# Attention logits of both maps made together, each map in its own 64 rows of the PE array

## The chip, the cores and the metric

One core of one Trainium2 chip runs the whole program. The metric is device time in microseconds. Engines are named as in the profile: PE is TensorE (with PEld, its weight loads), DVE is VectorE, ACT is ScalarE, POOL is GpSimd, SP issues most DMAs.

## The reference, cut to what matters

A two-layer trunk over 1024 tokens of width 1024. The change touches the second layer's differential attention: 8 heads, each with two maps (r = 0, 1) of 64 dimensions and values of 128.

```python
def diff_attention(qkv, q_gain, k_gain, lam_params, sub_gain, lam_init):
    q = rms_norm(q.reshape(bsz, seq, C_HEADS, 2, 64), q_gain) * 64 ** -0.5
    k = rms_norm(k.reshape(bsz, seq, C_HEADS, 2, 64), k_gain)
    v = v.reshape(bsz, seq, C_HEADS, 128)
    ...
        logits = einsum('bqhrd,bkhrd->bhrqk', q_blk, k) - slopes * dist    # blocks of 128 queries
        probs = softmax(where(dist >= 0, logits, -inf), axis=-1)
        attn = probs[:, :, 0] - lam * probs[:, :, 1]
        return einsum('bhqk,bkhe->bqhe', attn, v)
    ...
    o = rms_norm(o, sub_gain) * (1.0 - lam_init)
```

Everything is float32. The logits and the projections are made from float32 numbers that are split in two parts, `hi` (rounded to the type float32r, which PE multiplies in one pass) and `lo` (the rest), with the product of the two `lo` parts left out.

## The kernel before

The program is one stream: the first layer's mixing stage, its MLP and gate, then `attention` (L872 on), then the output projection and the second MLP. A scheduler of the framework orders each engine's instructions from the program's dependencies and from simulated times. An engine's queue is then fixed, and it runs in order.

`attention` walks through 8 heads of 8 blocks of 128 queries, 64 blocks in all, plus two iterations to drain. Block `b` of a head sees `n = (b + 1) * 128` keys, in one chunk of up to 512 columns for b < 4 and in two (512 and the rest) for b > 3: 96 chunks for each map. In iteration g of the loop the source issues

- `logits(0)` of block g, then `combine` of block g-1,
- `transpose` of block g-2, `logits(1)` of block g, `value` of block g-2,

with a call of `pump` between them. `pump` issues units of the work that fills PE meanwhile: the projections for later heads (tile `mm`), and near the end a part of the output projection (`mix_part`).

**Parts of q and k.** `put_k` transposes 512 keys (both maps stand one above the other in the 128 rows of `pt`) and writes for each map r a tile of 128 rows: `hi` in the map's own 64 rows, `lo` in the other 64 (L969 on ACT, L970 on DVE, 64 rows each). `put_q` does the same for 256 queries, but puts `hi` in both halves of `qh` (L980 on ACT, copied across by L981 on DVE), and `lo` in the own half of `ql` (L982 on DVE), whose other half was set to zero once (L947).

**Logits.** So each chunk of a map takes two matmuls over all 128 rows into one PSUM tile `qk`: `qh` with `ks` gives hi·hi + hi·lo, and `ql` with `ks` gives lo·hi. L1016 on DVE adds the bias `al`, writes `lg` and keeps the running extreme `nm`; L1019 on ACT takes the exponential and the sums.

**After the logits.** `combine` (L1025 to L1027, DVE) joins the two maps, `transpose` puts the result in `aT` by way of PSUM (L1037, ACT), `value` multiplies by v in `po` (L1047, L1049).

**PSUM** has four tags of two banks each here: `mm`, `tr`, `aux` and `sc`. The logits' tiles cycle through `aux`, `sc`, `aux`; `po` lives in `sc`.

All matmuls of this stage use the whole 128x128 array. The first layer's mixing stage, around 195 to 380 us, has small ones of 32*32 and 64*64 (tiles `py`, `pz`). A float32 product that isn't split (`po`, `tr`, `py`, `pz`) shows in the trace as two instructions.

Of the kernel before, what the change touches and what calls it, by code (L numbers as in the profile page):

```python
# [12 lines left out]
F32R = mybir.dt.float32r  # L13
AF = mybir.ActivationFunctionType
ALU = mybir.AluOpType
# [3 lines left out]
P = 128  # L19
# [4 lines left out]
HT = 512  # L24
# [15 lines left out]
def f32(ap):  # L40
    return ap.bitcast(F32)
# [73 lines left out]
class Trunk:  # L115
# [756 lines left out]
    def attention(self, w_qkv, w_out, gain_next, h_dram):  # L872

        nc = self.nc
        NB = NT
        hs, r = list(self.hs), list(self.r)
        self.mixed = [[None] * KT, [None] * KT]

        al = self.slot("B", [P, S], F32, "al")
# [62 lines left out]
        half = (slice(0, 64), slice(64, P))  # L942


        qlow = [self.slot(t, [P, 2, 2 * P], F32R, "ql") for t in ("c13", "d0")]
        for t in qlow:
            nc.vector.memset(f32(t), 0.0)  # L947

        lgs = [self.slot(f"A{4 + i}", [P, 2, S], F32, "lg") for i in range(2)]
        lg0 = [lgs[0][:, 0], lgs[0][:, 1], lgs[1][:, 0]]  # L950
        lg1 = lgs[1][:, 1]
        qk_tag = itertools.cycle(("aux", "sc", "aux"))
        aT_tag = itertools.cycle(("c8", "c9", "c10"))
        heads = {}

        def begin(hd):

            qk = qks[hd]

            ks = self.slot(f"A{2 + hd % 2}", [P, 2, S], F32R, "ks")  # L960

            def put_k(hf):
                pt = self.aux([P, HT], "tr", "tr")
                for t in range(4):
                    self.pe.transpose(pt[:, t * P : (t + 1) * P], qk[1][hf][:, t, :], self.ident)
                for r in range(2):
                    own, other = half[r], half[1 - r]
                    dst = ks[:, r, hf * HT : (hf + 1) * HT]
                    nc.scalar.activation(dst[own], pt[own], AF.Copy, scale=self.kg[own])  # L969
                    nc.vector.scalar_tensor_tensor(dst[other], pt[own], self.kg[own], f32(dst[own]), ALU.mult, ALU.subtract)  # L970

            def put_q(b2):
                pt = self.aux([P, HT], "tr", "tr")
                for i in range(2):
                    self.pe.transpose(pt[:, i * P : (i + 1) * P], qk[0][b2 // 2][:, 2 * (b2 % 2) + i, :], self.ident)
                qh = self.slot(f"c{11 + b2 % 2}", [P, 2, 2 * P], F32R, "qh")
                ql = qlow[b2 % 2]
                for r in range(2):
                    own, other = half[r], half[1 - r]
                    nc.scalar.activation(qh[own, r], pt[own, 0 : 2 * P], AF.Copy, scale=self.qg[own])  # L980
                    nc.vector.tensor_copy(qh[other, r], f32(qh[own, r]))  # L981
                    nc.vector.scalar_tensor_tensor(ql[own, r], pt[own, 0 : 2 * P], self.qg[own], f32(qh[own, r]), ALU.mult, ALU.subtract)  # L982
                return qh, ql

            put_k(0)
            heads[hd] = [ks, put_k, put_q, put_q(0)]

        class Block:
# [10 lines left out]
                me.sums, me.osq = heads[hd][4:6]  # L999
                me.nm = self.sp.tile([P, 2, 2], F32, tag="nm", name=self.nm("nm"))  # L1000

            def logits(me, r):
                hd, b, n, nm, lg = me.hd, me.b, me.n, me.nm, me.lg[r]
                if b == 0 and r == 0:
                    nc.vector.tensor_scalar(al, al, 0.5, None, ALU.mult)
                ks, _, _, (qh, ql) = heads[hd][:4]
                qs = slice((b % 2) * P, (b % 2 + 1) * P)
                nch = (n + HT - 1) // HT
                u0 = (NB - 1 - b) * P
                for c in range(nch):  # L1010
                    k0, k1 = c * HT, min(n, (c + 1) * HT)
                    ps = self.aux([P, HT], next(qk_tag), "qk")
                    self.pe.matmul(ps[:, : k1 - k0], lhsT=qh[:, r, qs], rhs=ks[:, r, k0:k1], start=True, stop=False)
                    self.pe.matmul(ps[:, : k1 - k0], lhsT=ql[:, r, qs], rhs=ks[:, r, k0:k1], start=False, stop=True)

                    nc.vector.tensor_tensor_reduce(  # L1016
                        out=lg[:, k0:k1], in0=ps[:, : k1 - k0], in1=al[:, u0 + k0 : u0 + k1], scale=-1.0,
                        scalar=3.0e38 if c == 0 else nm[:, r, 0:1], op0=ALU.add, op1=ALU.min, accum_out=nm[:, r, c : c + 1])
                nc.scalar.activation(lg[:, :n], lg[:, :n], AF.Exp, bias=nm[:, r, nch - 1 : nch], scale=-1.0, accum_out=me.sums[:, b, r : r + 1])  # L1019

            def combine(me):
                b, n, sums = me.b, me.n, me.sums
# [86 lines left out]
        def pump():  # L1109
            i = state[0] = state[0] + 1  # L1110
            for (i0, u0), (i1, u1) in zip(marks, marks[1:]):
                if i0 < i <= i1:
                    want = u0 + (u1 - u0) * (i - i0) / (i1 - i0)
                    while state[1] < want:
                        next(fill)
                        state[1] += 1
            if i > TAIL:
                next(tail, None)
# [12 lines left out]
        tail = tails()  # L1131
        blocks = []
        for g in range(8 * NB + 2):
            if g < 8 * NB:
                hd, b = divmod(g, NB)
                blocks.append(Block(hd, b))
                blocks[g].logits(0)
            if 0 < g <= 8 * NB:
                blocks[g - 1].combine()
            pump()  # L1140
            if g < 8 * NB and b % 2 and b < NB - 1:
                q = heads[hd][2]((b + 1) // 2)
            if g > 1:
                blocks[g - 2].transpose()
            pump()
            if g < 8 * NB:
                if b == 3 - (hd < 7):
                    heads[hd][1](1)
                blocks[g].logits(1)
            pump()  # L1150
            if g > 1:
                blocks[g - 2].value()
            pump()
            if g < 8 * NB:
                if b % 2 and b < NB - 1:
                    heads[hd][3] = q
                if b == 6 + (hd == 6) and hd < 7:
                    begin(hd + 1)
# [824 lines left out]
```

## Time and profile before

| what | value |
|---|---|
| median of 3 runs | 2536.98 us (2535.73 to 2537.92) |
| span of the profiled execution | 2535.2 us |
| PE / PEld / DVE / ACT busy, share of the span | 99% / 85% / 73% / 51% |
| granted TensorE clock, mean | 0.999 |

The span is the time from the first to the last instruction of one profiled execution; it lies 1.8 us under the median of the runs. In the rows of the trace, the first number after "x count" or the second of a timeline row is a duration; matmuls are pipelined, so that their durations overlap, and the distance between two starts tells what one costs. The form of a matmul's row is rows*columns of the array, then partitions x columns of its output.

### The profile page before, as it was taken

How to read it: one execution, taken by the hardware profiler on the slowest of the kernel's cores; microseconds unless marked ns; L12 is line 12 of the kernel's file. 1: busy time of each engine (PE TensorE's matmuls, PEld its weight loads, DVE VectorE, ACT ScalarE, POOL GpSimd, SP SyncE). 2: the span in 40 equal slices, each digit the busy share in tenths (PEclk: the TensorE clock that was granted, in tenths of full speed). 3: DMA queues.
4: the chain of work that ended last, by engine and by line, in shares of the span. 5: the costliest groups of instructions: out<-in, count | busy, mean ns of one | idle time of the engine just before them, and what ended most of it. 6: DMA issues, size and time to landing. Idle time of an engine off the chain costs nothing.

```text
span 2535.2 us, 40147 instructions
## 1 busy us (share of the span) xinstructions
PE 2515.3 (99%) x14046; PEld 2151.9 (85%) x14046; DVE 1854.3 (73%) x3676; ACT 1285.9 (51%) x2553; POOL 285.5 (11%) x256
## 2 busy tenths in 40 slices
PE   9999999999999999999999999999999999999999
PEld 7898898888888878888999999988778888888877
DVE  7867776697666888656477777787887677787586
ACT  6543444465455434544366666665654555445452
POOL 0301232000000000000334333310000000000000
PEclk9999999999999999999999999999999999999999
DMA  7452435457557756553211111147466558655651
GB/s 242 126 157 78 136 110 193 138 175 242 161 174 257 245 164 207 183 158 120 74 53 47 55 47 43 59 136 257 143 219 202 174 184 281 216 184 185 200 178 59
DMA packets 298818, 396.92 MB, mean 157 GB/s; under 512 B 37780, under 2 KB 165752, under 8 KB 298616
## 3 DMA queue, kind: packets, MB, share of 16 engines
q1 hardware_dynamic: 298600, 394.36, 48.4%
q8 instruction: 110, 1.80, 0.3%
q14 instruction: 92, 0.75, 0.1%
q10 hardware_dynamic: 16, 0.00, 0.0%
HBM read 289.40 MB, written 104.86 MB: 156 GB/s over the span
## 4 chain that ended last, share of the span: by engine, by line
PE 92%; DVE 4%; DMA 2%; issue 1%; ACT 1%; SPq 0%; POOL 0%; DVEq 0%; ACTq 0%; POOLq 0%
PE mm L76 79%; PE po L76 3%; PE qk L76 2%; PE aux L76 2%; PE tr L79 2%; DMA raw<-in_w_ple_gate_dram 1%; DVE lg L1016 0%; DVE w L224 0%; DMA raw<-in_w_mlp_dram 0%; PE pz L76 0%; PE py L76 0%; PE aux L79 0%; PE pvn L76 0%; PE pab L79 0%; PE pkq L76 0%
## 5 line engine op out<-in xcount | busy, mean ns | idle before, releaser
L76 PE MATMUL mm<-g,w 128*128 128x512 f32 x2592 | 603.6, 394 | 0.8 <-DVE g L224 0.5
L223 ACT CAST w<-raw 128x512 fp32r<-128x512 f32 x598 | 366.0, 618 | 453.8 <-PE mm L76 386.8
L76 PEld LDWEIGHTS mm<-g,w 128*128 128x128 f32 x2592 | 485.9, 188 | 116.2 <-DVE g L224 1.0
L76 PE MATMUL mm<-hi,w 128*128 128x512 f32 x1728 | 553.6, 396 | 0.3 <-ACT hi L1219 0.3
L76 PE MATMUL mm<-w,hi 128*128 128x256 f32 (+2 forms) x2528 | 505.5, 295 | 0.0
L224 DVE TENSOR_TENSOR w<-raw,w 128x512 fp32r<-128x512 f32 x534 | 364.8, 690 | 178.9 <-ACT w L223 169.4
L76 PEld LDWEIGHTS mm<-w,hi 128*128 128x128 f32 x2528 | 400.1, 188 | 13.6 <-DVE acc L284 0.3
L76 PEld LDWEIGHTS mm<-hi,w 128*128 128x128 f32 x1728 | 324.7, 188 | 73.7 <-ACT hi L1219 0.7
L76 PE MATMUL mm<-w,lo 128*128 128x256 f32 (+2 forms) x1264 | 370.3, 293 | 0.0
L76 PE MATMUL mm<-lo,w 128*128 128x512 f32 x864 | 341.6, 396 | 0.9 <-DVE lo L1220 0.9
L76 PE MATMUL mm<-t,w 128*128 128x512 f32 x1152 | 270.9, 394 | 1.2 <-ACT w L223 1.2
L76 PEld LDWEIGHTS mm<-t,w 128*128 128x128 f32 x1152 | 216.2, 188 | 52.8 <-ACT w L223 1.6
L76 PEld LDWEIGHTS mm<-w,lo 128*128 128x128 f32 x1264 | 238.2, 188 | 5.6
L76 PEld LDWEIGHTS mm<-lo,w 128*128 128x128 f32 x864 | 162.8, 188 | 36.8 <-DVE lo L1220 1.4
L224 DVE TENSOR_TENSOR g<-graw,g 128x512 fp32r<-128x512 f32 x216 | 147.2, 685 | 8.8 <-DMA gd<-g 6.9
L223 ACT CAST g<-graw 128x512 fp32r<-128x512 f32 x216 | 132.7, 617 | 32.8 <-issue 10.9
L1019 ACT ACTIVATE lg<-lg,nm 128x128 f32<-128x128 f32 (+7 forms) x128 | 99.5, 777 | 82.5 <-DVE nm L1016 76.0
L260 POOL TENSOR_TENSOR r<-ms,mhalf 128x4 f32<-128x4 f32 x12 | 13.3, 1109 | 1060.9 <-DVE ms L258 1033.5
L350 ACT ACTIVATE g<-g 128x512 f32<-128x512 f32 x96 | 60.6, 632 | 114.8 <-DVE g L284 114.5
L1016 DVE CUSTOM_DVE_ANT_0 lg<-qk,al 128x512 f32<-128x512 f32 (+3 forms) x128 | 75.1, 589 | 36.2 <-PE qk L76 32.8
L224 POOL TENSOR_TENSOR w<-raw,w 128x512 fp32r<-128x512 f32 x64 | 84.6, 1347 | 111.9 <-ACT w L223 63.0
L76 PE MATMUL mm<-ohi,w 128*128 128x512 f32 x256 | 85.2, 400 | 0.5 <-ACT ohi L1073 0.5
(336 smaller groups left out, 3612.4 us busy)
## 6 DMA issues: line engine op xcount, KB each, us to landing
raw<-in_w_mlp_dram SPq DMA_DIRECT2D x352, 256.0 KB, 3.3
graw<-gd SPq DMA_DIRECT2D x224, 256.0 KB, 2.8
gd<-g SPq DMA_DIRECT2D x192, 256.0 KB, 3.1
raw<-in_w_ple_gate_dram SPq DMA_DIRECT2D x76, 256.0 KB, 3.5
acc<-h_dram SPq DMA_DIRECT2D x64, 256.0 KB, 4.4
keep<-in_w_mlp_dram SPq DMA_DIRECT2D x64, 256.0 KB, 4.3
raw<-in_w_in_e_dram SPq DMA_DIRECT2D x60, 256.0 KB, 3.7
h_dram<-acc SPq DMA_DIRECT2D x48, 256.0 KB, 2.5
```

Source lines behind the costliest of these rows:

```text
L76: self._next(self.engine.matmul(*a, **k))
L79: self._next(self.engine.transpose(*a, **k))
L223: self.nc.scalar.copy(hi, src)
L224: (lo_engine or self.nc.vector).tensor_tensor(lo, src, f32(hi), ALU.subtract)
L260: nc.gpsimd.tensor_tensor(r, ms, self.mhalf[:, 0:4], ALU.pow)
L350: nc.scalar.activation(g, src, AF.Relu)
L1016: nc.vector.tensor_tensor_reduce(out=lg[:, k0:k1], in0=ps[:, : k1 - k0], in1=al[:, u0 + k0 : u0 + k1], scale=-1.0, scalar=3.0e38 if c == 0 ...
L1019: nc.scalar.activation(lg[:, :n], lg[:, :n], AF.Exp, bias=nm[:, r, nch - 1 : nch], scale=-1.0, accum_out=me.sums[:, b, r : r + 1])
```

## The change

The parts of q are kept once: `qs[:, 0]` has `hi` and `qs[:, 1]` `lo`, of both maps in the rows in which the transposes leave them; `ks[:, 0]` and `ks[:, 1]` the same for k. `put_k` and `put_q` make each part in one instruction over 128 rows. A logits chunk takes three matmuls for each map (hi·hi, hi·lo, lo·hi), each over the map's own 64 rows, the two maps alternating in the source, into two PSUM tiles, one of `aux` and one of `sc`. `logits` makes both maps of a block in one call, behind the `combine` of the block before.

```diff
-        qlow = [self.slot(t, [P, 2, 2 * P], F32R, "ql") for t in ("c13", "d0")]
-        for t in qlow:
-            nc.vector.memset(f32(t), 0.0)
...
-        qk_tag = itertools.cycle(("aux", "sc", "aux"))
+        qk_tag = itertools.cycle(("aux", "sc"))
...
             def put_k(hf):
...
-                for r in range(2):
-                    own, other = half[r], half[1 - r]
-                    dst = ks[:, r, hf * HT : (hf + 1) * HT]
-                    nc.scalar.activation(dst[own], pt[own], AF.Copy, scale=self.kg[own])
-                    nc.vector.scalar_tensor_tensor(dst[other], pt[own], self.kg[own], f32(dst[own]), ALU.mult, ALU.subtract)
+                hi, lo = (ks[:, i, hf * HT : (hf + 1) * HT] for i in range(2))
+                nc.scalar.activation(hi, pt, AF.Copy, scale=self.kg)
+                nc.vector.scalar_tensor_tensor(lo, pt, self.kg, f32(hi), ALU.mult, ALU.subtract)
 
             def put_q(b2):
...
-                qh = self.slot(f"c{11 + b2 % 2}", [P, 2, 2 * P], F32R, "qh")
-                ql = qlow[b2 % 2]
-                for r in range(2):
-                    own, other = half[r], half[1 - r]
-                    nc.scalar.activation(qh[own, r], pt[own, 0 : 2 * P], AF.Copy, scale=self.qg[own])
-                    nc.vector.tensor_copy(qh[other, r], f32(qh[own, r]))
-                    nc.vector.scalar_tensor_tensor(ql[own, r], pt[own, 0 : 2 * P], self.qg[own], f32(qh[own, r]), ALU.mult, ALU.subtract)
-                return qh, ql
+                q = self.slot(f"c{11 + b2 % 2}", [P, 2, 2 * P], F32R, "qs")
+                nc.scalar.activation(q[:, 0], pt[:, 0 : 2 * P], AF.Copy, scale=self.qg)
+                nc.vector.scalar_tensor_tensor(q[:, 1], pt[:, 0 : 2 * P], self.qg, f32(q[:, 0]), ALU.mult, ALU.subtract)
+                return q
...
-            def logits(me, r):
+            def logits(me):
...
                 for c in range(nch):
                     k0, k1 = c * HT, min(n, (c + 1) * HT)
-                    ps = self.aux([P, HT], next(qk_tag), "qk")
-                    self.pe.matmul(ps[:, : k1 - k0], lhsT=qh[:, r, qs], rhs=ks[:, r, k0:k1], start=True, stop=False)
-                    self.pe.matmul(ps[:, : k1 - k0], lhsT=ql[:, r, qs], rhs=ks[:, r, k0:k1], start=False, stop=True)
-
-                    nc.vector.tensor_tensor_reduce(...)
-                nc.scalar.activation(lg[:, :n], lg[:, :n], AF.Exp, ...)
+                    pss = [self.aux([P, HT], next(qk_tag), "qk") for _ in range(2)]
+                    for i, (x, y) in enumerate(((0, 0), (0, 1), (1, 0))):
+                        for r in range(2):
+                            self.pe.matmul(pss[r][:, : k1 - k0], lhsT=q[half[r], x, qs], rhs=ks[half[r], y, k0:k1], start=i == 0, stop=i == 2)
+                    for r in range(2):
+                        nc.vector.tensor_tensor_reduce(...)
+                for r in range(2):
+                    nc.scalar.activation(lg[r][:, :n], lg[r][:, :n], AF.Exp, ...)
...
         for g in range(8 * NB + 2):
+            if 0 < g <= 8 * NB:
+                blocks[g - 1].combine()
             if g < 8 * NB:
                 hd, b = divmod(g, NB)
                 blocks.append(Block(hd, b))
-                blocks[g].logits(0)
-            if 0 < g <= 8 * NB:
-                blocks[g - 1].combine()
+                blocks[g].logits()
             pump()
             if g < 8 * NB and b % 2 and b < NB - 1:
                 q = heads[hd][2]((b + 1) // 2)
             if g > 1:
                 blocks[g - 2].transpose()
             pump()
-            if g < 8 * NB:
-                if b == 3 - (hd < 7):
-                    heads[hd][1](1)
-                blocks[g].logits(1)
+            if g < 8 * NB and b == 3 - (hd < 7):
+                heads[hd][1](1)
             pump()
             if g > 1:
                 blocks[g - 2].value()
```

More of the change, by code (lines that the diff above doesn't have):

```diff
@@ L1000, in __init__ @@
                 me.nm = self.sp.tile([P, 2, 2], F32, tag="nm", name=self.nm("nm"))
-            def logits(me, r):
-                hd, b, n, nm, lg = me.hd, me.b, me.n, me.nm, me.lg[r]
-                if b == 0 and r == 0:
+            def logits(me):
+                hd, b, n, nm, lg = me.hd, me.b, me.n, me.nm, me.lg
+                if b == 0:
                     nc.vector.tensor_scalar(al, al, 0.5, None, ALU.mult)
-                ks, _, _, (qh, ql) = heads[hd][:4]
+                ks, _, _, q = heads[hd][:4]
                 qs = slice((b % 2) * P, (b % 2 + 1) * P)
@@ L1011, in logits @@
                     k0, k1 = c * HT, min(n, (c + 1) * HT)
-                    ps = self.aux([P, HT], next(qk_tag), "qk")
-                    self.pe.matmul(ps[:, : k1 - k0], lhsT=qh[:, r, qs], rhs=ks[:, r, k0:k1], start=True, stop=False)
-                    self.pe.matmul(ps[:, : k1 - k0], lhsT=ql[:, r, qs], rhs=ks[:, r, k0:k1], start=False, stop=True)
[L1016 to L1019, printed above, removed]
+                    pss = [self.aux([P, HT], next(qk_tag), "qk") for _ in range(2)]
[3 more added lines that the diff above has]
+                    for r in range(2):
+                        nc.vector.tensor_tensor_reduce(
+                            out=lg[r][:, k0:k1], in0=pss[r][:, : k1 - k0], in1=al[:, u0 + k0 : u0 + k1], scale=-1.0,
+                            scalar=3.0e38 if c == 0 else nm[:, r, 0:1], op0=ALU.add, op1=ALU.min, accum_out=nm[:, r, c : c + 1])
+                for r in range(2):
+                    nc.scalar.activation(lg[r][:, :n], lg[r][:, :n], AF.Exp, bias=nm[:, r, nch - 1 : nch], scale=-1.0, accum_out=me.sums[:, b, r : r + 1])
             def combine(me):
```

## The prediction

> **What bounds the kernel now.** First the head of the profile page: the span, busy times by engine, the granted clock, and the chain of work that ended last.
>
> ```profile
> span 2535.2 us, 40147 instructions
> PE 2515.3 (99%) x14046; PEld 2151.9 (85%) x14046; DVE 1854.3 (73%) x3676; ACT 1285.9 (51%) x2553; POOL 285.5 (11%) x256
> PEclk9999999999999999999999999999999999999999
> PE 92%; DVE 4%; DMA 2%; issue 1%; ACT 1%; SPq 0%; POOL 0%; DVEq 0%; ACTq 0%; POOLq 0%
> ```
>
> PE (TensorE) is busy in 99% of the span and is 92% of the chain; a change pays or costs by what it does to PE's own stream. The change lives in the attention stage alone. The logits' matmuls (tile `qk`) run from 1270.7 to 1720.4 us, so I take 1262 to 1745 us as the stage, in the view of stages, with PE's waits in that window from the view of waits.
>
> ```profile
> L76 PE MATMUL qk<-ks,qh x192: 219/392/483, 1270.7 to 1720.2; 128*128 128x512 f32 x96, 128*128 128x128 f32 x32, 128*128 128x256 f32 x32, 128*128 128x384 f32 x32
> L76 PE MATMUL qk<-ks,ql x192: 221/388/477, 1270.8 to 1720.4; 128*128 128x512 f32 x96, 128*128 128x128 f32 x32, 128*128 128x256 f32 x32, 128*128 128x384 f32 x32
> 1262.00:1745.00 483.00, 478.57 (x3681) 457.13 (x3680) 361.78 (x1034) 295.51 (x722) 157.02 (x129) 1.00 0.23 70
> PE tr L79 <- DVE olo L1074: 1.8, 3, 0.7
> PE qk L76 <- DVE nm L1016: 1.5, 2, 0.8
> ```
>
> In these 483 us PE is busy 478.57 (4.4 idle), the weight loader 457.13 (25.9 idle), VectorE only 361.78 and ScalarE 295.51. PE's waits on other engines are small; the two longest are shown. So relief on VectorE or ScalarE can buy at most the 25.9 us in which the loader rests, and more work on PE is paid in full: the projections and value products that PE runs between the logits are work that must be done anyway, not cover.
>
> **What a matmul costs.** Matmuls overlap their ends, so I read the price from start to start in the timeline, not from durations.
>
> ```profile
> 1452.63 0.34 PE L76 MATMUL qk<-ks,ql 128*128 128x384 f32 x1
> 1452.80 0.39 PE L76 MATMUL mm<-w,hi 128*128 128x256 f32 x2
> ...
> 1453.74 1.05 PE L76 MATMUL po<-v,aT 128*128 128x128 f32 x8
> ...
> 1457.18 0.40 PE L76 MATMUL qk<-ks,qh 128*128 128x512 f32 x1
> 1457.41 0.40 PE L76 MATMUL qk<-ks,ql 128*128 128x512 f32 x1
> 1457.65 0.39 PE L76 MATMUL mm<-w,hi 128*128 128x256 f32 x2
> 1457.88 0.28 PE L76 MATMUL mm<-w,lo 128*128 128x256 f32 x1
> ```
>
> 512 columns take 0.23 us to the next start (1457.18, 1457.41, 1457.65; I use 0.232), 384 take 0.175, 256 take 0.118 (two in 0.23), 128 take 0.112 (eight in 1.05, the last 0.27 of it one duration: 0.78/7). The 128-column price is that of one weight load, which otherwise hides behind the matmul before.
>
> **Logits before and after, on PE.** Before: 2 x 96 at 512 columns and 64 each at 384, 256 and 128: 192 x 0.232 + 64 x (0.175 + 0.118 + 0.112) = 70.5 us. After: three matmuls a map and chunk instead of two, 576 instead of 384, each in 64 of the 128 rows but with as many columns to stream: 1.5 x 70.5 = 105.7 us one behind another, 52.8 us if every matmul of one map ran beside one of the other.
>
> How many run side by side is decided by the order of issue. The source alternates the maps, but the scheduler orders PE's queue itself, and the built order of the changed kernel breaks the alternation. Three stretches of it:
>
> ```
> qk_13365 512, qk_13366 512, qk_13365 512, qk_13366 512, qk_13365 512, qk_13366 512, qk_13375 256 x3, mm ...
> qk_13468 512 x3, qk_13478 384 x3, mm x12, po x4, qk_13469 512 x3, tr ...
> mm ..., qk_13479 384 x3, mm ...
> ```
>
> qk_13365 and qk_13366 are the two maps of one chunk, and so are qk_13468 and qk_13469, here with 16 other matmuls between. Of the 96 chunks only 22 stand as six alternating matmuls; 32 have three of one map, other work, three of the other. Over all 576, 114 neighbours can be paired (62 at 512 columns, 15 at 384, 21 at 256, 16 at 128). These hide 62 x 0.232 + 15 x 0.175 + 21 x 0.118 + 16 x 0.112 = 21.3 us; letting a matmul start as soon as its own half is free, stretch by stretch, hides 22.1. So 105.7 - 22.1 = 83.6 us, 13.1 more than before.
>
> That neighbours in different rows do overlap I take from the small tiles of the other mixing stage, around 195 us and 206 us:
>
> ```profile
> 194.87 0.33 PEld L76 LDWEIGHTS py<-inv,am 32*32 32x32 f32 x16 [0.36 <-PE mm L76]
> 194.88 0.44 PE L76 MATMUL py<-inv,am 32*32 32x32 f32 x16
> ...
> 205.63 0.40 PE L76 MATMUL mm<-hi,w 128*128 128x512 f32 x1
> 205.96 0.54 PEld L76 LDWEIGHTS py<-xt,am 64*64 64x64 f32 x8 [0.36 <-issue]
> 205.96 0.67 PE L76 MATMUL py<-xt,am 64*64 64x64 f32 x8
> 206.56 0.19 PEld L76 LDWEIGHTS mm<-hi,w 128*128 128x128 f32 x1
> 206.57 0.51 PE L76 MATMUL mm<-hi,w 128*128 128x512 f32 x1
> 206.91 0.27 PE L76 MATMUL po<-state,qkv 128*128 128x128 f32 x1
> ```
>
> The eight 64*64 products all use the same rows and columns: their weight loads come every (0.54 - 0.13)/7 = 0.058 us, 0.029 for 32 columns. The sixteen 32*32 products alternate between two places: (0.33 - 0.11)/15 = 0.015 us each, so two at a time. These pairs differ in columns as well as rows; a pair in different rows and the same 128 columns, as here, no row shows. The bounds are 13.1 us more (full overlap) and 35.2 us more (none). I take full overlap, the nearest row.
>
> **The change of shape.** The same rows price what the source doesn't show: going from whole-array matmuls to matmuls in part of the array and back. The 512-column matmul that starts at 205.63 should give way at 205.86; the first small one starts at 205.96. Eight at 0.058 are 0.47 us. The whole-array matmul behind them starts at 206.57, but its follower only at 206.91, 0.34 later instead of 0.23: its weights were not loaded ahead, and it really streams from 206.68. From 205.86 to 206.68 are 0.82 us, less 0.47: 0.35 us lost for one trip in and out, part drain and part weight loads that no longer hide. Here the first load is for 128 columns instead of 64, 0.05 us more (by the 0.112 and 0.058): 0.40 where the neighbours have 256 columns or more, about 0.33 where they have 128 and the load is in the price already. I take 0.39. The bounds: 0.1, should a split in rows alone be cheaper, which no row shows or excludes, and 0.45.
>
> The rule that bears on it is in the Trainium skill, TensorEngine Tiling (Array Packing), Key Properties: changing the tiling mode, not only the tile, drains TensorE. The trace agrees, with the 0.35 us above; the page gives no figure. It speaks against this change, since the same page's Theoretical Speedup (up to 2x for a small dimension of 64 or less) assumes that such matmuls stay together.
>
> In the built order the 576 matmuls stand in 140 stretches with whole-array work between them: 71 are three matmuls long, 86 hold one map alone. 140 x 0.39 = 54.6 us.
>
> **Other engines.** Off the list go one of two 64-row instructions of every kind, and all copies of `qh`:
>
> ```profile
> L982 DVE SCALAR_TENSOR_TENSOR ql<-tr,qg,qh 64x256 fp32r<-64x256 f32 x63 | 30.5, 484 | 1.5
> L980 ACT ACTIVATE qh<-tr,qg 64x256 fp32r<-64x256 f32 x63 | 29.4, 467 | 22.0 <-PE tr L79 11.2 <-DVE ql L982 10.0
> L981 DVE CAST qh<-qh 64x256 fp32r<-64x256 f32 x63 | 25.7, 408 | 9.8 <-ACT qh L980 8.6
> L970 DVE SCALAR_TENSOR_TENSOR ks<-tr,kg,ks 64x512 fp32r<-64x512 f32 x32 | 24.0, 750 | 1.9 <-ACT ks L969 0.9
> L969 ACT ACTIVATE ks<-tr,kg 64x512 fp32r<-64x512 f32 x32 | 21.8, 682 | 9.7 <-PE tr L79 5.6 <-DVE ks L970 3.7
> L1016 DVE CUSTOM_DVE_ANT_0 lg<-qk,al 128x512 f32<-128x512 f32 x80 | 55.0, 688 | 19.0 <-PE qk L76 18.0
> ```
>
> VectorE: 64 x 0.408 + 32 x 0.484 + 16 x 0.750 = 53.6 us less; ScalarE: 32 x 0.467 + 16 x 0.682 = 25.9 us less (128 rows cost as 64 do: the time goes by columns). Both sit behind PE, so this is worth between nothing and the 25.9 us of loader rest; I take nothing, since PE's waits on them are the few shown. The combine of a block now stands ahead of the next block's logits on VectorE: the logits' reductions (L1016) queue behind it, and PE's next logits behind those, for their two PSUM tiles. With both maps open, a chunk asks for one tile of `aux` and one of `sc`, where `po` lives too. Cost between nothing and one 0.688 us eviction for a third of the 96 chunks, 22 us; I take nothing, since VectorE has 121 us free in the window. DMAs don't change.
>
> **Sum.** 13.1 + 54.6 = 67.7 us. The profiled execution spans 2535.2 us, 1.8 under the median of the runs, 2537.0; the same 1.8 us around the span holds after: 2535.2 + 67.7 + 1.8 = 2604.7. I predict 2605.
>
> **Rivals.**
>
> - *No overlap in the same columns.* For it: no row shows such a pair. Against it: the 0.015 us. 35.2 + 54.6 = 89.8: 2627. Chance 0.14.
> - *A new wait for the logits' tiles.* For it: `sc` is shared, and the scheduler already tears chunks apart. Against it: VectorE's free time. 67.7 + 22: 2627. Chance 0.08.
> - *The change of shape is cheap* in rows alone, 0.1 us: 13.1 + 14: 2564. Against it: 32*32 and 64*64 both show the gap. Chance 0.08.
> - *Faster.* The change of shape costs nothing and VectorE's 53.6 us were what kept the loader resting: 13.1 - 25.9 = -12.8: 2524. It decides where a trip costs under 12.8/140 = 0.09 us and all the rest goes. Chance 0.03.
> - *Every pair side by side*, trips free: 52.8 us for the logits, 17.7 less than before, 2519. Against it: the built order pairs 114 of 288. Chance 0.01. This is what the Trainium skill's 2x, TensorEngine Tiling (Array Packing), Theoretical Speedup, would make of it.
>
> **Numbers.** The forecast has 0.65; 0.01 is left for a price of a trip just around 0.09 us, within 0.2% of before, which is about what a measurement can tell from no change. Faster 0.04 (the last two rivals), same 0.01, slower 0.95. The forecast's own bounds (0.33 to 0.45 us a trip) are 2596 to 2613; the range takes in the first two rivals and their spread above, and half-way to the cheap change below: 2575 to 2636.
>
> **What would show it.** In the profile after: the stage from 1262 us takes about 551 us instead of 483, and nothing before it moves; neighbouring `qk` matmuls of the two maps start together (0.23 us a pair at 512 columns, 0.46 if not); the `qk` weight loads show 0.3 us and more of idle time before a stretch, and so do the loads right behind one; VectorE's share of the stage falls. A stage under 500 us, or gaps of under 0.1 us around the stretches, would prove the working wrong.

## The result and the profile after

The changed kernel takes 2595.08 us (median of 4 runs, 2593.98 to 2596.27) against 2537.45 us (4 runs, 2535.73 to 2538.91): ratio 1.0227, 95% interval 1.0212 to 1.0241. It is 57.6 us slower; the forecast was 2605, 67.7 slower.

The head of the page after, then the view of stages, first of before and then of after, each up to the end of the value products, and the rows of the copy out of `po` that give that end:

```profile
span 2593.0 us, 40390 instructions
PE 2575.2 (99%) x14238; PEld 2165.6 (84%) x14238; DVE 1801.1 (69%) x3562; ACT 1256.9 (48%) x2505; POOL 288.6 (11%) x256
PE 95%; DVE 2%; DMA 1%; issue 1%; POOL 0%; ACT 0%; SPq 0%; DVEq 0%; POOLq 0%; ACTq 0%
```

```profile
0.00:1262.00 1262.00, 1254.15 (x6918) 1061.03 (x6919) 904.29 (x1694) 605.58 (x1158) 121.45 (x120) 1.00 0.53 168
1262.00:1744.00 482.00, 477.57 (x3677) 456.32 (x3676) 360.81 (x1031) 295.34 (x722) 157.02 (x129) 1.00 0.23 70
L1047 DVE COPY o<-po x64: 271/291/295, 1284.8 to 1743.3; 128x128 f32<-128x128 f32 x64
```

```profile
0.00:1262.00 1262.00, 1253.21 (x6907) 1059.91 (x6908) 900.20 (x1689) 604.18 (x1157) 124.81 (x120) 1.00 0.53 168
1262.00:1802.00 540.00, 538.09 (x3875) 470.57 (x3874) 311.25 (x922) 267.44 (x672) 156.79 (x129) 1.00 0.20 63
L1039 DVE COPY o<-po x64: 278/291/293, 1286.5 to 1801.7; 128x128 f32<-128x128 f32 x64
```

Up to 1262 us nothing of note has moved (PE 1254.15 and 1253.21 us busy). The last copy out of `po` starts at 1801.7 instead of 1743.3: the attention stage is 58.4 us longer, which is the whole loss. In it PE counts as busy to 2 us (538.09 of 540), while the weight loader now rests 69 us of it (540 - 470.57) instead of 26 (482 - 456.32). VectorE does 50 us less, and the stage is no shorter for it.

PE's waits, from 1262 to 1800 us, were seven rows before, 5.6 us together. After, the view has a single row:

```profile
PE tr L79 <- issue: 1.8, 1, 1.8
```

How the logits look now, in the timeline of PE (start, length, instruction, count):

```profile
1299.89 0.36 PE L76 MATMUL mm<-w,hi 128*128 128x256 f32 x1
1300.10 0.28 PE L76 MATMUL mm<-w,lo 128*128 128x256 f32 x1
1300.31 1.32 PE L76 MATMUL qk<-ks,qs 64*128 64x512 f32 x9
1301.55 0.51 PE L76 MATMUL mm<-w,hi 128*128 128x256 f32 x2
...
1310.83 0.50 PE L76 MATMUL po<-v,aT 128*128 128x128 f32 x3
...
1311.25 0.96 PE L76 MATMUL qk<-ks,qs 64*128 64x512 f32 x3
1312.14 0.66 PE L79 MATMUL tr<-ident,lg 128*128 128x128 f32 x4
```

The nine at 1300.31 are six of 512 columns, the maps alternating, and three of 256 of one map. The 256-column matmul at 1300.10 should give way at 1300.22; the pair at 1301.55 runs 0.51 instead of the usual 0.40, so its first really streams from 1301.66 (1301.55 + 0.51 - 0.40). From 1300.22 to 1301.66 are 1.44 us; three pairs of 0.232 and three singles of 0.118 are together 1.05. So the six of 512 columns ran as three, and 0.39 us went on the way in and out. The stretch at 1311.25 has three of one map alone and takes as long as three.

Done for every stretch (from where the matmul before should give way, to where the first one behind really streams), the logits take 74.4 us in 153 stretches before and 133.4 us in 140 stretches after: 59.0 more. Everything else together is 1.4 us the other way (57.6 - 59.0).

The 74.4 us are not all streaming. By the prices of the prediction the logits before stream 70.5 us, and 150 of the 153 stretches keep to these prices (0.1 us over them together). The other 3.9 us lie in three stretches in which PE waits, 1.6, 1.5 and 0.8 us. The first of them, in the kernel before:

```profile
1378.79 0.39 PE L76 MATMUL qk<-ks,qh 128*128 128x256 f32 x1
1379.02 0.28 PE L76 MATMUL qk<-ks,ql 128*128 128x256 f32 x1
1380.05 0.36 PE L76 MATMUL qk<-ks,qh 128*128 128x256 f32 x1 [0.76 <-DVE nm L1016]
```

After a matmul of 256 columns at 1379.02 the next should start at 1379.14; it starts at 1380.05.

### The profile page after: what moved, and what is told of

It reads as the page before. It is cut to its first block, busy times and chain, and to the rows that moved or that the text cites. A ratio compares the mean times of both kernels' runs of the same rounds, so it can differ in the third digit from the quotient of the medians.

```text
span 2593.0 us, 40390 instructions
## 1 busy us (share of the span) xinstructions
PE 2575.2 (99%) x14238; PEld 2165.6 (84%) x14238; DVE 1801.1 (69%) x3562; ACT 1256.9 (48%) x2505; POOL 288.6 (11%) x256
## 4 chain that ended last, share of the span: by engine, by line
PE 95%; DVE 2%; DMA 1%; issue 1%; POOL 0%; ACT 0%; SPq 0%; DVEq 0%; POOLq 0%; ACTq 0%
PE mm L76 80%; PE qk L76 4%; PE po L76 3%; PE tr L79 2%; PE aux L76 2%; DMA raw<-in_w_mlp_dram 0%; PE pz L76 0%; PE py L76 0%; PE pvn L76 0%; PE pkq L76 0%; PE pst L76 0%; PE pks L76 0%; PE aux L79 0%; DMA guv<-uv_dram 0%; POOL al L881 0%
## 5 line engine op out<-in xcount | busy, mean ns | idle before, releaser
L76 PE MATMUL mm<-w,hi 128*128 128x256 f32 (+2 forms) x2528 | 512.7, 298 | 0.0
L76 PEld LDWEIGHTS mm<-t,w 128*128 128x128 f32 x1152 | 216.2, 188 | 52.8 <-ACT w L223 1.6
L1011 ACT ACTIVATE lg<-lg,nm 128x256 f32<-128x256 f32 (+7 forms) x128 | 99.0, 774 | 67.7 <-DVE nm L1007 65.7
L76 PE MATMUL qk<-ks,qs 64*128 64x512 f32 (+3 forms) x576 | 116.4, 373 | 0.1
```

What stands on the lines that cost most here:

```text
L76: self._next(self.engine.matmul(*a, **k))
L1011: nc.scalar.activation(lg[r][:, :n], lg[r][:, :n], AF.Exp, bias=nm[:, r, nch - 1 : nch], scale=-1.0, accum_out=me.sums[:, b, r : r + 1])
```

## The experiments

Two theories were set against each other. One is the forecast's: matmuls in different rows run side by side, and each stretch costs a trip into the split shape and back. The rivals: the trip is free and the time goes on waits for the logits' PSUM tiles; or pairs don't overlap.

**1. The same order, all rows.**

```diff
-  self.pe.matmul(pss[r]..., lhsT=q[half[r], x, qs], rhs=ks[half[r], y, k0:k1], ...)
+  self.pe.matmul(pss[r]..., lhsT=q[:, x, qs], rhs=ks[:, y, k0:k1], ...)
```

> The changed kernel with every logits matmul over all 128 rows instead of the map's own 64 (so both maps' logits are summed into each tile: the output is not the reference's). The same 576 matmuls of the same columns stand in the same order on PE, so there is no change of shape and nothing runs side by side. Theory (shape changes cost, pairs overlap): the logits' stretches take 105.7 us of streaming plus the usual 4 us, against 133.4 now: 2595 - 24 to 28 = 2567 to 2571. Rival (the time went into waits for the logits' PSUM tiles): the waits stay and the overlap goes, 2595 or more, up to 2617.

Measured 2568.9 us, ratio 1.0128 (1.0098 to 1.0157) to before: 26 us faster than the changed kernel although nothing runs side by side. The logits' stretches take 106.0 us; the plain sum is 105.7, which leaves nothing for waits for their tiles. So the rival of new waits in the changed kernel is out. The kernel is 32.0 us slower than before, where the prices alone give 105.7 - 70.5 = 35.2: some 3 us of the waits before are gone (1.7 us of them left in PE's view of waits instead of 5.6). The relief of VectorE and ScalarE is in this kernel too, but run 2 below loses the same waits without it.

**2. The trip by itself, in the kernel before.**

```diff
-  self.pe.matmul(ps..., lhsT=ql[:, r, qs], rhs=ks[:, r, k0:k1], start=False, stop=True)
+  self.pe.matmul(ps..., lhsT=ql[half[r], r, qs], rhs=ks[half[r], r, k0:k1], start=False, stop=True)
```

> The kernel before, in which only the second matmul of each map and chunk (lo of q with hi of k, the other half of its rows are zeros) is taken over the map's own 64 rows. The order on every engine is that of before, no matmul is added, nothing is made together. 192 such matmuls make 184 trips into the split shape and back. Theory: 184 x 0.36 us = 67 us slower, 2604, though nothing else has changed. Rival (rows alone don't cost a change of shape, the loss in the changed kernel is waiting): 2537.

Measured 2602.0 us, ratio 1.0258 (1.0228 to 1.0288), 65.1 us slower for 184 trips: 0.35 us each, net. By the starts its logits take 139.7 us, 69.2 more than the 70.5 of streaming: 0.38 us a trip. The difference of 4 us fits the waits of the kernel before, which are gone: PE's view of waits has 1.4 us instead of 5.6, though nobody is relieved here. A part of its timeline on PE, and one row of the weight loader's:

```profile
1500.42 0.40 PE L76 MATMUL qk<-ks,qh 128*128 128x512 f32 x1
1500.75 0.49 PE L76 MATMUL qk<-ks,ql 64*128 64x512 f32 x1
1501.17 0.39 PE L76 MATMUL qk<-ks,qh 128*128 128x256 f32 x1
1501.48 0.39 PE L76 MATMUL qk<-ks,ql 64*128 64x256 f32 x1
1501.80 0.50 PE L76 MATMUL mm<-w,hi 128*128 128x256 f32 x2
...
1500.74 0.18 PEld L76 LDWEIGHTS qk<-ks,ql 64*128 64x128 f32 x1 [0.25 <-issue]
```

`ql` in 64 rows starts 0.33 us after `qh` instead of 0.23, is itself longer (0.49 for 0.40; its weights load only as it starts, at 1500.74), and the matmul behind it waits again. A split in rows alone costs the trip in full, with the same arithmetic in the same order. The rival of a cheap trip is out.

**3 and 4. PE in the order of the source; the two maps apart.** Both kernels add, for the attention loop, an edge from each PE instruction to the one before it, so the scheduler can't reorder PE. The fourth also swaps the two inner loops.

```diff
     def _next(self, inst):
-        self.mark = inst.ins.name
+        last, self.mark = self.mark, inst.ins.name
+        if self.strict:
+            self.behind(inst, last)
```

```diff
-                    for i, (x, y) in enumerate(((0, 0), (0, 1), (1, 0))):
-                        for r in range(2):
+                    for r in range(2):
+                        for i, (x, y) in enumerate(((0, 0), (0, 1), (1, 0))):
```

> The changed kernel with PE's instructions of the attention loop held in the order of the source: each block's logits stand as one stretch, the two maps alternating (64 stretches instead of 140, all 288 pairs side by side). Theory: 52.8 + 64 x 0.364 = 76.1 us for the logits instead of 133.4: 2595 - 57 = 2538, if the fixed order adds no waits. Rival (waits for the logits' tiles): a block of two chunks asks for four PSUM tiles at once, 32 blocks wait for evictions of 0.69 us and the projections no longer fill the gap: 2560 or more.

> As the ordered kernel, but in each chunk the three matmuls of one map stand before the three of the other: the same 64 stretches and the same instructions, with one overlapping pair at each seam. Theory (matmuls in different rows and the same 128 columns overlap): 105.7 - 17.6 (seams in a chunk) - 5.1 (seams between two chunks) = 83.0 us of streaming instead of 52.8: 30 us slower than the ordered kernel, about 2568. Rival (they don't overlap): the same as the ordered kernel, both near 2591.

The third took 2577.1 us (1.0160, 1.0130 to 1.0189) and not 2538. Its 64 stretches do take only 80.7 us, near the 76.1. Of the 39 us by which it misses, some 24 are PE waiting elsewhere (25.4 us in the view of waits, 1.8 in the changed kernel), first for `aT`:

```profile
PE po L79 <- ACT aT L1032: 9.8, 13, 1.4
PE tr L82 <- ACT aT L1032: 8.0, 9, 3.0
```

The rest is not assigned. The granted clock, 1.00 from 1600 to 1800 us in the kernel before, is 0.97 and 0.98 in the two halves of that time here; no run separates what that costs.

The fourth took 2587.0 us (1.0199, 1.0169 to 1.0228), 10 us more than the third instead of 30, and both theories missed what it showed. Its stretches take 82.2 us, as with alternation. Timeline of PE, the third kernel and then the fourth; the last row is from a window that ends 0.14 us into the fourth's stretch:

```profile
1298.28 0.28 PE L79 MATMUL mm<-w,lo 128*128 128x256 f32 x1
1298.49 1.32 PE L79 MATMUL qk<-ks,qs 64*128 64x512 f32 x12
1299.74 0.50 PE L79 MATMUL mm<-w,hi 128*128 128x256 f32 x2
```

```profile
1299.95 0.28 PE L79 MATMUL mm<-w,lo 128*128 128x256 f32 x1
1300.16 1.32 PE L79 MATMUL qk<-ks,qs 64*128 64x512 f32 x12
1301.41 0.50 PE L79 MATMUL mm<-w,hi 128*128 128x256 f32 x2
...
1300.16 0.51 PE L79 MATMUL qk<-ks,qs 64*128 64x512 f32 x2
```

The same twelve matmuls, six of 512 and six of 256 columns, take 1.32 us in both. In the fourth the second to start does so 0.01 us after the first (two take 0.51 together, the first alone 0.50). The next two in the queue are of the first one's map, whose rows it holds for 0.23 us, so the second is the other map's first matmul: PE starts it ahead of two that stand before it. So overlap in the same columns is shown, and it doesn't need the maps to alternate. Why the fourth loses 8 us more outside the stretches is open.

**5 and 6. Stretches kept whole, the scheduler free otherwise.** The first matmul of a stretch waits until the PSUM tiles are free (`free` has the last readers of `aux` and `sc`), and the stretch then goes first. The sixth also makes the logits of blocks 0 and 1, and of 2 and 3, in one stretch, in buffers of their own.

```diff
+                free = [x for u in reads.values() for y in u[-2:] for x in y]
...
+                with self.tc.high_priority(EARLY):
...
+                                if last:
+                                    self.pe.behind(inst, last)
+                                else:
+                                    for x0 in free:
+                                        self.tc.add_manual_dep(inst.ins, x0, sync, reason="tiles free")
```

> The changed kernel, scheduler free as before, but the first logits matmul of a block waits until all the PSUM tiles that the block may need are free, and the block's matmuls then go ahead of other work: 65 stretches instead of 140, nothing else held. Theory (a stretch costs 0.36 us whatever it holds, all pairs overlap): 52.8 + 65 x 0.364 = 76.5 us for the logits instead of 133.4: 2595 - 57 = 2538, up to 2543 if the 4 us by which the ordered kernel's stretches (80.7) missed their sum stay. Rival (logits in one piece bring waits on evictions, whoever orders the rest): as the kernel in source order, 2577.

> As the joined kernel, and the logits of blocks 0 and 1, and of 2 and 3, of a head in one stretch, with buffers of their own for the second block: 49 stretches. Theory: 52.8 + 49 x 0.364 = 70.6 us against 74.4 in the kernel before: 2533, up to 2538 with the 4 us of the ordered kernel; the even point lies at (74.4 - 52.8) / 0.364 = 59 stretches. Rival (waits on evictions): 2560 and more.

The fifth took 2554.4 us (1.0068, 1.0051 to 1.0085), the sixth 2548.0 us (1.0042, 1.0027 to 1.0057). The logits do nearly as the price of a trip says: 78.0 us in 65 stretches (76.5 expected), 73.6 us in 49 (70.6 expected). That is 0.8 under the 74.4 of the kernel before, but 3.1 over the 70.5 that its logits stream. The whole misses its sum by 10 us and more in both, so part of the rival holds: whole stretches bring waits for others. By the starts, PE's gaps of over 0.15 us outside the logits' stretches add up, to the last value product, to 11.3 us in the fifth and 11.4 in the sixth, against 2.9 before; in the fifth some 5 us of its loss stay unassigned. PE's longest waits in the sixth:

```profile
PE po L76 <- DVE nm L1026: 3.3, 5, 0.9
PE tr L81 <- DVE ks L970: 1.6, 3, 0.8
PE tr L81 <- DVE olo L1089: 1.6, 2, 1.0
```

In the first row `po` waits for the reductions of the logits (L1026), which share the banks of `sc`. That the bursts of logits delay the other two as well is likely, but not shown.

**7 and 8. Two controls on the kernel before.** The seventh puts the edges of the third on the kernel before. The eighth makes both maps together behind `combine`, with tiles alternating between `aux` and `sc`, and keeps doubled parts and whole-array matmuls:

```diff
+            if 0 < g <= 8 * NB:
+                blocks[g - 1].combine()
             if g < 8 * NB:
...
                 blocks[g].logits(0)
-            if 0 < g <= 8 * NB:
-                blocks[g - 1].combine()
+                blocks[g].logits(1)
...
-                blocks[g].logits(1)
```

> The kernel before, with PE held to the order of the source in the attention loop as in the ordered kernel; whole-array logits. It tells whether the 39 us by which the ordered kernel missed its sum (2577 for 2538) belong to the split rows or to the fixed order. If to the fixed order: 2537 + 25 to 45 = 2562 to 2582. If to the split rows: 2537 to 2545.

> The kernel before with one part of the change alone: both maps' logits of a block issued together behind the combine of the block before, tiles alternating between aux and sc; whole-array matmuls with doubled parts as before. Theory: PE's work is the same, so 2537 within 4 us. Rival (making both maps at once costs waits that the relief on VectorE and ScalarE hid in the run with full rows): 2545 or more.

The seventh took 2596.4 us (1.0233, 1.0212 to 1.0253): a fixed order alone costs the kernel before 59 us, so a loss like the third kernel's 39 us needs no split rows. That all of the 39 belong to the order is argued and not shown, since PE's longest wait is another one here:

```profile
PE tr L82 <- DVE ks L973: 26.1, 10, 4.9
```

The eighth took 2537.5 us (0.9997, 0.9986 to 1.0007): making both maps together changes nothing, and PE's view of waits has 5.3 us (5.6 before).

**9. How far PE looks.** In a block of two chunks, all six matmuls of map 0 stand before all six of map 1:

```diff
-                for c in range(nch):
...
-                        for r in range(2):
+                for r in range(2):
+                    for c, k0, k1, pss in chunks:
+                        for i, (x, y) in enumerate(((0, 0), (0, 1), (1, 0))):
```

> As the ordered kernel, but a block of two chunks issues all six matmuls of map 0 (both chunks) and then all six of map 1. In the kernel with three of one map before three of the other, twelve matmuls of 512 and 256 columns took the same 1.32 us as in alternation, so PE itself starts a matmul of the other half of the rows ahead of two that stand before it. If it looks five ahead as well: again 1.32 us for such a stretch, the stretches near 82 us in all. If it looks only a few ahead: the second map starts later, by up to 0.23 us x 3 and more at 512 columns, the stretches up to 82 + 32 x 0.7 = 104 us. If strictly in order: 32 stretches of two chunks without overlap, 120 us.

Measured 2592.0 us (1.0216, 1.0195 to 1.0236), the stretches 99.2 us: the middle case. One of 512 and 256 columns in the timeline, whole and cut off 0.52, 0.57 and 0.58 us after its start:

```profile
1302.98 1.89 PE L79 MATMUL qk<-ks,qs 64*128 64x512 f32 x12
...
1302.98 0.72 PE L79 MATMUL qk<-ks,qs 64*128 64x512 f32 x2
...
1302.98 0.96 PE L79 MATMUL qk<-ks,qs 64*128 64x512 f32 x3
...
1302.98 1.07 PE L79 MATMUL qk<-ks,qs 64*128 64x512 f32 x4
```

It takes 1.89 us instead of 1.32. The second matmul starts only 0.33 us after the first and the third 0.57 us; both are of map 0. The fourth to start is map 1's first, 0.008 us after the third, that is with three of map 0 still waiting ahead of it. It is so in all 32 stretches of two chunks, 0.006 to 0.008 us after the third start, whatever the width of the second chunk; a wait for a PSUM tile would not end so evenly. In the fourth kernel two waited ahead and it started at once.

**10. `po` in other banks.** On the sixth kernel, because of its longest wait. Two things change with it: a stretch no longer waits for the readers of `po`, and each chunk multiplies its three products in the reverse order.

```diff
-                po = self.aux([P, P], "sc", "po")
+                po = self.aux([P, P], "tr", "po")
```

> As the kernel with 49 stretches, but the value product's tile po moves from the banks of sc, which the logits of two chunks fill, to those of tr, and each chunk starts with the product that needs the part made last; 51 stretches. In the kernel with 49 stretches the logits took 73.6 us, 0.8 less than in the kernel before, and the 10 us by which it is slower lie in other waits of PE. If the wait of po for the evictions of the logits is the main one: 2537 to 2541. If the waits come from elsewhere (bursts of evictions on VectorE, transposes now waiting for po): 2546 to 2552.

Measured 2574.2 us (1.0142, 1.0125 to 1.0159), worse than either case: the logits take 70.3 us in 51 stretches, but PE's view of waits has 26.1 us (10.8 in the sixth). The longest:

```profile
PE mm L76 <- DVE k L925: 6.5, 4, 3.4
PE po L76 <- ACT aT L1051: 6.1, 10, 0.7
PE tr L81 <- ACT t L1063: 5.1, 3, 2.4
```

The transposes now wait for `po` to be read (the last row). As three things were changed, the run doesn't tell which of them brought the other two waits. No version tried beats the kernel before.

## Why the prediction was right, point by point

- *What bounds the kernel* held. The loss is PE's, in the attention stage alone. By the pages, VectorE is busy 48 us less and ScalarE 30 us less in run 1 than before, and nothing shows that this bought time there, as taken.
- *Overlap in the same columns* held, the bound of 13.1 and not that of 35.2 us. The count of pairs was too low: it let matmuls start in the order of the queue, but PE looks past matmuls of the same half. With the halves independent inside a stretch, the built order streams 81.1 us, not 83.6; looking past three gives the same sum.
- *The change of shape* held at 52.3 us (133.4 - 81.1), 0.37 us for each of the 140 trips; taken were 54.6 us at 0.39. The second kernel, with trips and nothing else, gives 0.38 by the starts. The nearest row was of another shape, so the fit could not be known.
- *The logits before* were rightly priced at 70.5 us; the 74.4 us in place hold 3.9 us of waits.
- *Waits taken at nothing* is the largest term of the miss. The prediction asked what new waits the change would bring and what relief would save, and let the waits of the kernel before stand. They went: the 3.9 us in its logits, and 1.4 us elsewhere. Run 2 loses them with no relief, so a PE that itself takes longer is enough to explain it.

The 10.1 us of the miss are these terms: 5.3 (waits gone) + 2.5 (pairs) + 2.3 (trips). All three have the same sign, so none hid another; together they put the result about 1 us under the forecast's own bounds (2596 to 2613), which had no term for waits that go. The lower end of the range, 2575, is not half-way to the cheap change at 2564 (that would be 2580 from 2596), but nothing hangs on it.

Of the signs, the stage took 540 us for the 551 that were forecast, and pairs do start together. The idle time of the weight loads came out smaller than the 0.3 us: in the median 0.13 us before a stretch and 0.25 us behind it. The price of a trip was right, not the way it shows there.

Of the rivals, the cheap trip and the missing overlap are excluded by runs 2 and 4, new waits in the changed kernel by run 1 and by its view of waits; the two in which the kernel gets faster, by the result. Waits do come, but only where the order is fixed or the stretches are made whole (runs 3 to 7, 9 and 10).

## What to carry to other kernels

Splitting the array by rows can pay only over a stretch long enough to earn its way in and out: a trip cost as much here as 1.6 matmuls of 512 columns. The even point lies at (70.5 - 52.8) / 0.37 = 48 stretches, an estimate from the figures above, and 64 blocks with one stretch each are already too many. (The 59 in the expectation of run 6 counts the waits of the kernel before as time of its logits.) The order in which the scheduler will issue has to be read from the built program before such a change is priced: here it tore 64 possible stretches into 140. Forcing them whole brought other waits of PE, 8.5 us more in runs 5 and 6, and neither came under the kernel before. And a kernel's small waits are worth looking at one by one: they can vanish when the engine that waits gets slower, and then a loss comes out smaller than its parts.

## What the runs showed of the hardware that was not expected

The description of the kernel before says that an engine's queue runs in order. PE didn't start matmuls strictly in the order of its queue: where the halves of the rows differ, one was started ahead of two others 0.01 us after the first (run 4), and in run 9 only once three were left ahead of it, 0.57 us later. Moving a float32r matmul from 128 rows to 64 made no difference to its stream: 0.23 us at 512 columns from the second start to the third in run 9, as with 128.
